# An encoder layer's second feed-forward projection: token-major Strassen products from streamed operands, with some operands stored as two planes

## The chip, the core and the metric

The kernel runs on one core of a Trainium2 chip. The metric is device time in microseconds (us) of one execution, input and output in the chip's memory (HBM). Engines: TensorE (PE) does matmuls into PSUM, VectorE (DVE), ScalarE (ACT) and GpSimd (POOL) do elementwise work, SyncE (SP) issues nearly all DMAs. Each engine works through its own instructions in a fixed order; an instruction waits on semaphores for what it needs, and everything behind it on that engine waits with it.

## What is computed

One layer of an encoder, float32, 2048 tokens of 1024 features, 16 query heads and 4 key heads, window of 128, hidden size 2816:

```python
h = rmsnorm(x, mix_norm_pre) * (1 + sc1) + sh1
y = windowed_gqa_sink(h, w_qkv, w_o, sink, rel_bias)
x = x + g1 * rmsnorm(y, mix_norm_post)
h = rmsnorm(x, ffn_norm_pre) * (1 + sc2) + sh2
a, b = split(h @ w_in, 2);  y = (silu(a) * b) @ w_out
x = x + g2 * rmsnorm(y, ffn_norm_post)          # rmsnorm: y * rsqrt(mean(y*y, -1) + eps) * gain
```

The change is about the last two lines: the product with `w_out` (2816 x 1024) and the norm, gain and residual behind it. `x` on the right of the last line is the result of the attention part, kept in HBM as `x1_d`.

## The kernel before

Matmuls take operands in a rounded 32-bit form (`fp32r`). For full precision each operand is split: `split` lets ScalarE copy it to the rounded high part and VectorE subtract that from the original to get the low part (lines 149 and 150). A product is then three matmuls, high x high, high x low, low x high (`three`, lines 144 to 146). A matmul has a stationary operand of 128x128 and a moving one of up to 128x512, and fills a PSUM buffer of 128x512.

The feed-forward part works by Strassen's scheme with seven products for 2x2 blocks. The two halves of 1024 tokens (`hf` 0 and 1) are two chunks of 512 tokens each (`CPH` = 2), and these are the two columns of the blocks.

*First projection (hidden phase).* For every half and 22 blocks of `w_in` (`Hidden`, names ending `_i0_t`, `_i1_t`) seven products of 12 matmuls go to PSUM tiles `pc0` to `pc6` of the pool `psC`, which has six buffers. ScalarE copies product 0 to `p1`; VectorE adds the others into `u2`, `p1`, `u3`, `b1` (lines 803 to 822). Then SiLU (line 828) and a product on GpSimd (line 832) give the hidden activations. Two neighbouring blocks are a pair (11 a half); `give_pair` forms the seven right-hand Strassen operands of the pair (`b11`, `b21`, `b22` as they are, `t1` to `t4` by two subtractions on GpSimd and two on VectorE) and stores each as 128x512 floats in `g_d`. The temporaries come from a pool of ten buffers, `tmp`. In half 0 the last two blocks are done product by product in turn (`interleaved`), while the operands of half 1 (`hb..`, `ht..`) are loaded and split as those of half 0 come free. The raw `w_in` tiles, their four sums on GpSimd (`s1` to `s4`) and the splits (`wa..`, `ws..`) are made a block or two ahead.

*Second projection.* It is cut along the hidden dimension into parts, `PARTS`: of each half four parts with 2, 3, 3, 3 and 3, 3, 3, 2 pairs, written (hf, part). The class `Outs` does all parts but the last: `w_out` is the stationary operand and the activations move, so the output has features on partitions. The part's activation operands are loaded from `g_d` and split (names like `hb21o0_1_0`), and for each of four pairs of feature blocks (`n2`) the rows `wiro` of `w_out` are loaded, their sums made and split. Product i goes to `pc{i}_o..` in `psC`; in a half's first part ScalarE copies it to a sum tile `z` (line 960), later VectorE adds it (line 963). In the half's last Strassen part the seven sums are combined (`COMBINE`, line 967). The last part, (1,3), is done without Strassen (`pl`, 96 matmuls with 512 columns and 192 with 256). The norm squares on ScalarE (line 993), adds squares on GpSimd or VectorE (line 994), sums over features by matmuls with ones, and multiplies (line 1010) and adds the residual (line 1011, `zx`).

The order on every engine is set when the kernel is built, by a scheduler that takes the program's order as its priority, with `tc.high_priority` moving pieces earlier. The last hidden block does its steps 0 to 4, then the first loads of the second projection are put in with high priority, then its steps 5 and 6.

## Time and profile before

| | us |
|---|---|
| runs | 2222.78, 2218.33, 2224.84 (median 2222.78) |
| profiled execution | 2223.03 |
| its span, first to last instruction | 2221.2 |
| VectorE, ScalarE, GpSimd busy | 1619.7, 1083.4, 1226.4 |
| mean granted TensorE clock | 0.967 of full speed |

All times below are from the profiled execution, counted from the span's start. In groups of instructions a line reads: line, engine, operation, tile written and tiles read, shapes, count, then total busy time and mean ns of one, then how long its engine was idle before it and what ended that. A row of a window gives its span, then the busy time of each engine with the number of instructions. The second projection runs from about 1724 to the end.

### The profile page before, as it was taken

The page shows a single profiled execution, that of the slowest core. Times are in us where ns is not written, and L with a number is a line of the kernel's source. Part 1 is how long each engine was busy: PE and PEld are TensorE (multiplying, and loading weights), DVE is VectorE, ACT ScalarE, POOL GpSimd, SP SyncE. Part 2 cuts the span into 40 slices and gives each one's busy share as a digit, 9 for nine tenths or more (in the row PEclk, how much of TensorE's full clock was granted, in tenths as well). Part 3 has the DMA queues.
Part 4 walks back from the last instruction along what each step waited for, and adds up shares of the span by engine and source line. Part 5 has one row for each costly group of instructions (what it writes and reads, how often), then busy time and mean ns, then how long its engine had stood idle before and what let it go on. Part 6 is the DMA issues. An engine that isn't in the chain of part 4 may idle for free.

```text
span 2221.2 us, 29169 instructions
## 1 busy us (share of the span) xinstructions
PE 2072.4 (93%) x9366; PEld 1672.9 (75%) x9366; DVE 1619.7 (73%) x2546; ACT 1083.4 (49%) x2153; POOL 1226.4 (55%) x1093
## 2 busy tenths in 40 slices
...
GB/s 260 236 263 302 259 172 220 147 209 167 182 207 157 181 216 99 174 143 152 158 184 172 241 189 114 103 106 105 89 101 79 206 157 151 119 105 256 161 128 100
DMA packets 263493, 375.97 MB, mean 169 GB/s; under 512 B 86011, under 2 KB 138796, under 8 KB 261292
## 3 DMA queue, kind: packets, MB, share of 16 engines
...
q10 hardware_dynamic: 576, 0.52, 0.1%
HBM read 263.37 MB, written 110.66 MB: 168 GB/s over the span
## 4 chain that ended last, share of the span: by engine, by line
PE 32%; DVE 8%; DMA 4%; issue 3%; POOL 3%; ACT 1%; SPq 0%; DVEq 0%; POOLq 0%; ACTq 0%
PE pc_i L145 6%; PE pc_i L144 6%; PE pc_i L146 6%; PE pc_o L145 4%; PE pc_o L144 4%; PE pc_o L146 4%; DMA wiri<-w_in 1%; DVE z L963 1%; DVE zx L1011 1%; DVE ws_o L150 1%; DMA ly<-y_d 1%; POOL z L967 1%; DMA lh<-x_d 1%; DVE ly L522 0%; DVE z L967 0%
## 5 line engine op out<-in xcount | busy, mean ns | idle before, releaser
L144 PE MATMUL pc_i<-ht,ws_i 128*128 128x512 f32 x528 | 208.6, 395 | 1.6 <-DVE u_i L806 0.9
L146 PE MATMUL pc_i<-ht,ws_i 128*128 128x512 f32 x528 | 207.2, 392 | 0.0
L145 PE MATMUL pc_i<-ht,ws_i 128*128 128x512 f32 x528 | 207.0, 392 | 0.0
L459 POOL TENSOR_SCALAR pr<-pr,rs 128x288 f32<-128x288 f32 (+3 forms) x256 | 138.5, 561 | 66.9 <-DVE rs L457 61.6
L453 DVE CUSTOM_DVE_ANT_0 pr<-s,bias,nsink 128x288 f32<-128x288 f32 (+3 forms) x256 | 123.8, 499 | 66.1 <-PE s L450 54.0
L455 ACT ACTIVATE pr<-pr,nm 128x289 f32<-128x289 f32 (+3 forms) x256 | 135.5, 532 | 73.6 <-DVE nm L453 63.7
L150 DVE TENSOR_TENSOR wa_i<-wiri,wa_i 128x512 fp32r<-128x512 f32 x132 | 135.1, 1024 | 38.9 <-ACT wa_i L149 33.3
L832 POOL TENSOR_TENSOR p_i<-p_i,u_i 128x512 f32<-128x512 f32 x44 | 69.9, 1589 | 168.3 <-DVE u_i L819 106.9
L150 DVE TENSOR_TENSOR ws_i<-s_i,ws_i 128x512 fp32r<-128x512 f32 x132 | 128.5, 973 | 27.4 <-ACT ws_i L149 25.7
L149 ACT CAST ws_i<-s_i 128x512 fp32r<-128x512 f32 x132 | 81.7, 621 | 134.2 <-PE pc_i L146 126.3
L145 PE MATMUL pc_i<-hb,wa_i 128*128 128x512 f32 x352 | 140.0, 398 | 2.6 <-DVE hb L150 2.6
L146 PE MATMUL pc_i<-hb,wa_i 128*128 128x512 f32 x352 | 140.2, 398 | 2.0 <-DVE wa_i L150 2.0
L144 PE MATMUL pc_i<-hb,wa_i 128*128 128x512 f32 x352 | 141.0, 400 | 0.4 <-DVE b_i L816 0.4
L149 ACT CAST wa_i<-wiri 128x512 fp32r<-128x512 f32 x132 | 81.9, 621 | 118.3 <-PE pc_i L146 115.8
L450 PE MATMUL s<-k,q 128*128 128x288 f32 (+4 forms) x512 | 116.4, 327 | 19.8 <-DVE nm L453 19.5
L472 PE MATMUL t<-ident,pr 128*128 128x128 f32 x736 | 119.0, 285 | 14.4 <-DVE plo L150 6.0
L150 DVE TENSOR_TENSOR plo<-t,phi 128x512 fp32r<-128x512 f32 x184 | 122.1, 683 | 14.1 <-ACT phi L149 12.9
L144 PEld LDWEIGHTS pc_i<-ht,ws_i 128*128 128x128 f32 x528 | 99.8, 189 | 24.5 <-DVE u_i L806 1.4
L450 PEld LDWEIGHTS s<-k,q 128*128 128x128 f32 x512 | 88.0, 201 | 39.3 <-DVE nm L453 28.8
L146 PEld LDWEIGHTS pc_i<-ht,ws_i 128*128 128x128 f32 x528 | 99.4, 188 | 23.2
L472 PEld LDWEIGHTS t<-ident,pr 128*128 128x128 f32 x736 | 92.7, 146 | 32.0 <-POOL pr L462 7.7
L145 PEld LDWEIGHTS pc_i<-ht,ws_i 128*128 128x128 f32 x528 | 99.4, 188 | 22.6 <-DVE ht L150 0.4
...
## 6 DMA issues: line engine op xcount, KB each, us to landing
...
q_d<-eq SPq DMA_DIRECT2D x64, 256.0 KB, 4.9
q<-q_d SPq DMA_DIRECT2D x16, 1024.0 KB, 6.1
...
g_d_b<-p_i SPq DMA_DIRECT2D x44, 256.0 KB, 4.9
```

What stands on the lines that cost most here:

```text
L144: pe.matmul(ps, w[0], h[0], start=first, stop=False)
L145: pe.matmul(ps, w[0], h[1], start=False, stop=False)
L146: pe.matmul(ps, w[1], h[0], start=False, stop=last)
L149: act.copy(hi, src)
L150: return eng.tensor_tensor(lo, src, f(hi), ALU.subtract).ins
L450: m = pe.matmul(ps[:, :n], qs, kk[:, e, jb * P + lo:jb * P + hi], start=e == 0, stop=e == 1)
L453: dve.tensor_tensor_reduce(pr[:, i, lo:hi], ps[:, :n], bias[g][:, lo - starts[i]:hi - starts[i]], -1.0, nsink[:, g:g + 1], ALU.add, ALU.mi ...
L455: act.activation(pr[:, i, lo:hi + 1], pr[:, i, lo:hi + 1], AF.Exp, bias=nm[:, i:i + 1], scale=-1.0, accum_out=rs[:, i:i + 1])
L459: pool.tensor_scalar(pr[:, i, lo:hi], pr[:, i, lo:hi], rs[:, i:i + 1], 1.0, ALU.mult, ALU.mult)
L472: pe.transpose(pt[:, i * P:(i + 1) * P], pr[:, i, jj * P:(jj + 1) * P], ident)
L832: pool.tensor_tensor(sa, sa, b, ALU.mult)
L963: dve.tensor_tensor(q, ps, q, ALU.add)
```

## The change

What it does:

- `give_pair` stores 14 of the 22 pairs (parts (0,3) and all of half 1, `SPLIT`) as two planes, high and low. For each of a pair's seven operands ScalarE now makes the high part (`gh..`) and VectorE the low part (`gl..`, or in place), in the hidden phase, and two DMAs store them; the tiles come from the same ten buffers. The second projection then loads both planes in one DMA and does not split them. The other eight pairs are stored and split as before.
- All eight parts go by Strassen, and the last pair of blocks is interleaved in both halves. The steps 5 and 6 of the last hidden block no longer lie between the loads.
- The activations are the stationary operand (128 tokens) and the `w_out` blocks move (512 features), so a PSUM tile `po` holds tokens on partitions. `Weights.put` loads a pair's rows of `w_out` as one tile of 1 MB (`wr`), makes the sums on GpSimd and splits them; the raw tile has one buffer for each of the three pairs. `Grams.load` streams the activations into 15 buffers, product by product. Order: part, product, token block b; in the last part token block, then product.
- Norm: ScalarE squares with an accumulated sum along the row (`ss`), a few short operations on 128x2 numbers give the factor `r`, and one VectorE operation multiplies with `r` and the gain row `grow`. The residual `x1` is loaded as it is and turned by 16 TensorE transposes for a token block (`px`); a VectorE addition ends it. `out` is written token-major.

The diff, cut to its core (the removed class `Outs`, the removed last part and the old norm are left out):

```diff
+SPLIT = ((0, 3), (1, 0), (1, 1), (1, 2), (1, 3))
...
-    g_d = [[{n: dram.tile([P, CH], F32, name=f"g_d{i}_{j}_{n}") for n in OPERANDS + ("b12",)}
+    part_of = [[(p, k) for p, m in enumerate(PARTS[i]) for k in range(m)] for i in range(S // HALF)]
+    g_d = [[{n: dram.tile([P, 2 if (i, part_of[i][j][0]) in SPLIT else 1, CH], F32, name=f"g_d{i}_{j}_{n}") for n in OPERANDS}
...
     def give_pair(hf, j):
         b = {f"b{e + 1}{i + 1}": hidden.pop((2 * j + e, i)) for e in range(2) for i in range(CPH)}
-        def give(n, t):
-            sp.dma_start(g_d[hf][j][n], t)
-        if hf == S // HALF - 1 and j >= HT // 2 - PARTS[-1][-1]:
-            for n in b:
-                give(n, b[n])
-        else:
-            differences(b["b11"], b["b12"], b["b21"], b["b22"], give)
+        parted = (hf, part_of[hf][j][0]) in SPLIT
+        def give(n, t, keep):
+            d = g_d[hf][j][n]
+            if not parted:
+                sp.dma_start(d[:, 0], t)
+                return
+            hi = temp(f"gh{hf}_{j}_{n}").bitcast(F32R)
+            lo = (temp(f"gl{hf}_{j}_{n}") if keep else t).bitcast(F32R)
+            split(hi, lo, t, dve)
+            sp.dma_start(d[:, 0], f(hi))
+            sp.dma_start(d[:, 1], f(lo))
+        b11, b12, b21, b22 = (b[n] for n in ("b11", "b12", "b21", "b22"))
+        give("b11", b11, True)
+        pool.tensor_tensor(b11, b12, b11, ALU.subtract)
+        dve.tensor_tensor(b12, b22, b12, ALU.subtract)
+        give("t3", b12, False)
+        give("b22", b22, True)
+        pool.tensor_tensor(b22, b22, b11, ALU.subtract)
+        give("t1", b11, False)
+        give("b21", b21, True)
+        dve.tensor_tensor(b21, b21, b22, ALU.subtract)
+        give("t2", b22, False)
+        give("t4", b21, False)
...
-        for t in range(HT - 2 if hf + 1 < S // HALF else HT - 1):
+        for t in range(HT - 2):
...
+        pair = [Hidden(half, t, hf) for t in range(HT - 2, HT)]
+        half = None
         if hf + 1 < S // HALF:
-            pair = [Hidden(half, t, hf) for t in range(HT - 2, HT)]
...
-            interleaved(pair, half)
-    hid = Hidden(half, HT - 1, hf)
-    for i in range(5):
-        hid.step(i)
+        interleaved(pair, half)
     early.close()
...
+    ffn.close()
+    psc.close()
...
+    PRODUCTS = (("s1", "t1", "5"), ("a12", "b21", "2"), ("a11", "b11", "1"), ("s2", "t2", "6"),
+                ("a22", "t4", "4"), ("s3", "t3", "7"), ("s4", "b22", "3"))
+    SUMS = {"1": (("2", "1", pool),), "6": (("6", "1", dve), ("1", "6", "5", pool)),
+            "7": (("7", "6", dve), ("4", "7", pool), ("5", "7", dve)), "3": (("3", "1", dve),)}
...
+    WB, GB, G0 = 14, 15, 5
...
+    psO = open_pool(ctx, "psO", 6, space=PSUM)
+    parts = [(hf, p) for hf in range(S // HALF) for p in range(len(PARTS[hf]))]
+    stages = [(part, i) for part in parts for i in range(len(PRODUCTS))]
+    class Weights:
+        def __init__(self):
+            self.at, self.n, self.src, self.w = 0, 0, [], {}
+        def load(self, hf, p):
+            self.src = []
+            for k in range(PARTS[hf][p]):
+                u = f"{hf}_{p}_{k}"
+                j = sum(PARTS[hf][:p]) + k
+                raw = rp.tile([P, 2, 2, CH], F32, tag=f"raw{k}", name=f"wr{u}")
+                sp.dma_start(raw, a["w_out"][2 * j:2 * j + 2].rearrange("e p (i c) -> p e i c", i=2))
+                a11, a12, a21, a22 = [raw[:, e, i] for i in range(2) for e in range(2)]
+                s1 = rp.tile([P, CH], F32, tag=f"s{k}", name=f"ws{u}")
+                pool.tensor_tensor(s1, a21, a22, ALU.add)
+                pool.tensor_tensor(a21, a11, a21, ALU.subtract)
+                self.src.append(dict(a11=a11, a12=a12, a22=a22, s1=s1, s2=s1, s3=a21, s4=a12))
+        def put(self, n=1):
...
+                (hf, p), i = stages[self.at]
+                self.at += 1
+                if i == 0:
+                    self.load(hf, p)
+                name = PRODUCTS[i][0]
+                for k, src in enumerate(self.src):
+                    t = wo.tile([P, 2, CH], F32R, tag=f"w{self.n % WB}", name=f"wo{hf}_{p}_{name}_{k}")
+                    self.n += 1
+                    split(t[:, 0], t[:, 1], src[name], dve)
+                    self.w[hf, p, i, k] = t
+                    if name == "s1":
+                        pool.tensor_tensor(src["s2"], src["s1"], src["a11"], ALU.subtract)
+                    elif name == "a12":
+                        pool.tensor_tensor(src["s4"], src["a12"], src["s2"], ALU.subtract)
+    class Grams:
+        def __init__(self):
+            self.at, self.n, self.g = 0, G0, {}
+        def load(self, n=1):
...
+                (hf, p), i = stages[self.at]
+                self.at += 1
+                for k in range(PARTS[hf][p]):
+                    d = g_d[hf][sum(PARTS[hf][:p]) + k][PRODUCTS[i][1]]
+                    t = gp.tile([P, 2, CH], F32R, tag=f"g{self.n % GB}", name=f"g{hf}_{p}_{i}_{k}")
+                    self.n += 1
+                    if (hf, p) in SPLIT:
+                        sp.dma_start(f(t), d)
+                    else:
+                        sp.dma_start(f(t[:, 1]), d[:, 0])
+                        split(t[:, 0], t[:, 1], f(t[:, 1]), dve)
+                    self.g[hf, p, i, k] = t
...
+    def product(hf, p, i, b):
+        m, name = PARTS[hf][p], PRODUCTS[i][2]
+        ps = psO.tile([P, CH], F32, tag="p", name=f"po{hf}_{p}_{i}_{b}")
+        for k in range(m):
+            g, w = grams.g[hf, p, i, k][:, :, b * P:(b + 1) * P], wts.w[hf, p, i, k]
+            pe.matmul(ps, g[:, 0], w[:, 0], start=k == 0, stop=False)
+            pe.matmul(ps, g[:, 0], w[:, 1], start=False, stop=False)
+            pe.matmul(ps, g[:, 1], w[:, 0], start=False, stop=k == m - 1)
+        if p == 0:
+            z[hf, b, name] = yp.tile([P, CH], F32, tag="z", name=f"z{hf}_{b}_{name}", bufs=28)
+            act.copy(z[hf, b, name], ps)
+        else:
+            dve.tensor_tensor(z[hf, b, name], ps, z[hf, b, name], ALU.add)
+        if p == len(PARTS[hf]) - 1:
+            for x, *y, eng in SUMS.get(name, ()):
+                y = [x] + y if len(y) == 1 else y
+                eng.tensor_tensor(z[hf, b, x], z[hf, b, y[0]], z[hf, b, y[1]], ALU.add)
...
+    def finish(hf, b):
+        x1, ss = {}, yp.tile([P, 4], F32, tag="ss", name=f"ss{hf}_{b}", bufs=2)
+        for j in range(CPH):
+            x1[j] = yp.tile([P, KT, P], F32, tag="x1", name=f"x1_{hf}_{j}_{b}", bufs=2)
+            sp.dma_start(x1[j], x1_d[hf * CPH + j][:, :, b * P:(b + 1) * P])
+            for i in range(2):
+                sq = yp.tile([P, CH], F32, tag="sq", name=f"sq{hf}_{j}_{b}_{i}", bufs=1)
+                act.activation(sq, z[hf, b, PLACE[i, j]], AF.Square, accum_out=ss[:, i * 2 + j:i * 2 + j + 1])
+        yield
...
+        yield
+        for j in range(CPH):
+            for i in range(2):
+                y = z[hf, b, PLACE[i, j]]
+                px = psF.tile([P, CH], F32, tag="mm", name=f"px{hf}_{j}_{b}_{i}")
+                for k in range(JB):
+                    pe.transpose(px[:, k * P:(k + 1) * P], x1[j][:, i * JB + k, :], ident)
+                dve.scalar_tensor_tensor(y, y, r[:, j:j + 1], grow[:, i * CH:(i + 1) * CH], ALU.mult, ALU.mult)
+                dve.tensor_tensor(y, px, y, ALU.add)
+                sp.dma_start(out[hf * CPH + j, b, :, i * CH:(i + 1) * CH], y)
...
+    wts, grams = Weights(), Grams()
...
+        grams.load(4)
+        wts.put(4)
...
+    for hf, p in parts[:-1]:
+        for i in range(len(PRODUCTS)):
+            for b in range(JB):
+                product(hf, p, i, b)
+                next(end, None)
+            wts.put()
+            grams.load()
+        if p == len(PARTS[hf]) - 1:
+            end = chain(*(finish(hf, b) for b in range(JB)))
+    for b in range(JB):
+        for i in range(len(PRODUCTS)):
+            product(*parts[-1], i, b)
+            if b == 0:
+                wts.put()
+                grams.load()
+            next(end, None)
+        end = chain(end, finish(parts[-1][0], b))
+    for _ in end:
+        pass
```

What the scheduler makes of it. First, ScalarE at the seam between the halves: `p1_i0_20` is the copy of product 0 of half 0's block 20, `gh0_9_..` are high parts of pair 9 (blocks 18 and 19), `hb111_..` operands of half 1. Before:

```order
L828 ACTIVATE u2_i0_19_11993<-u2_i0_19_11993 128x512
L803 COPY p1_i0_20_12180<-pc0_i0_20_12167 128x512
L149 CAST wa11_i1_0_12514<-wiri1_0_12504 128x512
L803 COPY p1_i0_21_12195<-pc0_i0_21_12182 128x512
L149 CAST wa11_i1_1_12652<-wiri1_1_12642 128x512
L149 CAST ws2_i1_0_12517<-s2_i1_0_12508 128x512
L149 CAST hb111_0_12197<-hb111_0_12197 128x512
L149 CAST hb111_1_12201<-hb111_1_12201 128x512
```

and now:

```order
L152 CAST gh0_9_t1_12102<-p1_i0_18_11828 128x512
L152 CAST gh0_9_b21_12107<-p1_i0_19_11988 128x512
L152 CAST hb111_0_12238<-hb111_0_12238 128x512
L152 CAST wa11_i1_1_12724<-wiri1_1_12714 128x512
L152 CAST hb111_1_12242<-hb111_1_12242 128x512
L152 CAST ws2_i1_0_12589<-s2_i1_0_12580 128x512
L152 CAST gh0_9_t2_12114<-u2_i0_19_12003 128x512
L152 CAST gh0_9_t4_12119<-p1_i0_19_11988 128x512
L152 CAST ws2_i1_1_12727<-s2_i1_1_12718 128x512
L152 CAST hb111_2_12246<-hb111_2_12246 128x512
L152 CAST hb111_3_12250<-hb111_3_12250 128x512
L823 COPY p1_i0_20_12221<-pc0_i0_20_12208 128x512
```

The copy now stands behind the last of pair 9's high parts and four operands of half 1; before, it stood ahead of these operands.

Second, ScalarE at the start of the second projection, around its first copies out of PSUM (`z`). Before, with `wa..`, `ws..` parts of the third group of rows `wiro0_0_2`:

```order
L149 CAST wa11_o0_0_2_15924<-wiro0_0_2_15914 128x256
L149 CAST hb22o0_0_0_15749<-hb22o0_0_0_15749 128x512
L149 CAST hb22o0_0_1_15753<-hb22o0_0_1_15753 128x512
L149 CAST ws2_o0_0_2_15927<-s2_o0_0_2_15918 128x256
L960 COPY z0_0_0_15764<-pc0_o0_0_0_15757 128x512
L960 COPY z0_0_1_15773<-pc1_o0_0_0_15766 128x512
L960 COPY z0_0_2_15782<-pc2_o0_0_0_15775 128x512
L960 COPY z0_0_3_15791<-pc3_o0_0_0_15784 128x512
```

and now, with `gh1_10_..` high parts of the very last pair, `g0_1_..` operands of part (0,1), and `wo0_1_s1_..` that part's first sums of `w_out`:

```order
L152 CAST gh1_10_t4_16069<-p1_i1_21_15846 128x512
L1085 ACT_TABLE_LOAD
L152 CAST g0_1_0_1_16392<-g0_1_0_1_16392 128x512
L152 CAST wo0_1_s1_0_16376<-ws0_1_0_16363 128x512
L152 CAST g0_1_0_2_16396<-g0_1_0_2_16396 128x512
L152 CAST wo0_1_s1_1_16380<-ws0_1_1_16368 128x512
L1050 COPY growt_16171<-pgrow_16169 8x128
L1036 COPY z0_0_5_16182<-po0_0_0_0_16175 128x512
L1036 COPY z0_1_5_16191<-po0_0_0_1_16184 128x512
L1036 COPY z0_2_5_16200<-po0_0_0_2_16193 128x512
```

The copies now stand behind pieces that belong to the next part. The raw tiles that `wo0_1_s1_0` and `wo0_1_s1_1` come from are loaded into the buffers of part (0,0), `wr0_0_0` and `wr0_0_1`, after VectorE has split the last sum made there, and the load of `wr0_0_0` itself waits for the last matmul of the hidden phase, whose operands lay in that room. On SyncE the loads of `wr0_1_0` and `wr0_1_1` stand behind the stores of pair 10's planes.

Third, VectorE at the end of the program. Before:

```order
L136 TENSOR_TENSOR nrz3_256_19994<-nrz3_256_19994,ntz3_256_20004 128x256
L1010 TENSOR_TENSOR z1_0_6_17941<-z1_0_6_17941,nrz3_256_19994 128x256
L1010 TENSOR_TENSOR z1_1_6_18126<-z1_1_6_18126,nrz3_256_19994 128x256
L1010 TENSOR_TENSOR z1_2_6_18426<-z1_2_6_18426,nrz3_256_19994 128x256
L1010 TENSOR_TENSOR z1_3_6_18438<-z1_3_6_18438,nrz3_256_19994 128x256
L1011 SCALAR_TENSOR_TENSOR zx3_0_19651<-z1_0_6_17941,coef_336,zx3_0_19651 128x256
L1011 SCALAR_TENSOR_TENSOR zx3_1_19669<-z1_0_4_17897,coef_336,zx3_1_19669 128x256
L1011 SCALAR_TENSOR_TENSOR zx3_2_19688<-z1_1_6_18126,coef_336,zx3_2_19688 128x256
L1011 SCALAR_TENSOR_TENSOR zx3_4_19742<-z1_2_6_18426,coef_336,zx3_4_19742 128x256
L1011 SCALAR_TENSOR_TENSOR zx3_3_19717<-z1_1_4_18082,coef_336,zx3_3_19717 128x256
```

and now:

```order
L1072 TENSOR_TENSOR r1_3_19955<-r1_3_19955,t1_3_19956 128x2
L1080 SCALAR_TENSOR_TENSOR z1_3_2_18169<-z1_3_2_18169,r1_3_19955,grow_16097 128x512
L1080 SCALAR_TENSOR_TENSOR z1_3_4_18504<-z1_3_4_18504,r1_3_19955,grow_16097 128x512
L1080 SCALAR_TENSOR_TENSOR z1_3_3_18633<-z1_3_3_18633,r1_3_19955,grow_16097 128x512
L1080 SCALAR_TENSOR_TENSOR z1_3_5_18050<-z1_3_5_18050,r1_3_19955,grow_16097 128x512
L1081 TENSOR_TENSOR z1_3_2_18169<-px1_0_3_0_19965,z1_3_2_18169 128x512
L1081 TENSOR_TENSOR z1_3_4_18504<-px1_0_3_1_19973,z1_3_4_18504 128x512
L1081 TENSOR_TENSOR z1_3_3_18633<-px1_1_3_0_19981,z1_3_3_18633 128x512
L1081 TENSOR_TENSOR z1_3_5_18050<-px1_1_3_1_19989,z1_3_5_18050 128x512
```

The last token block's four scaled tiles and four residual additions from PSUM now end the program, where there were pieces of 256 columns scaled and added.

189 lines of the change are left out of this document (38 added, 151 removed).

## The prediction

> **What bounds the kernel now.** I read the page first, then windows by stage, then the groups and the chain of waits at the places that the change touches.
>
> ```profile
> span 2221.2 us, 29169 instructions
> PE 2072.4 (93%) x9366; PEld 1672.9 (75%) x9366; DVE 1619.7 (73%) x2546; ACT 1083.4 (49%) x2153; POOL 1226.4 (55%) x1093
> PE 32%; DVE 8%; DMA 4%; issue 3%; POOL 3%; ACT 1%; SPq 0%; DVEq 0%; POOLq 0%; ACTq 0%
> ```
>
> TensorE is busy 93% of the span and has the largest share of the chain that ended last, so what can change is the 149 us in which it is not busy, and the number of matmuls. By window the columns are: us, TensorE busy (matmuls), weight loads, VectorE, ScalarE, GpSimd, granted clock, DMA share, GB/s.
>
> ```profile
> 1250.00:1270.00 20.00, 20.00 (x88) 16.20 (x87) 13.62 (x15) 7.86 (x14) 16.31 (x13) 1.00 0.83 271
> 1270.00:1320.00 50.00, 44.42 (x178) 34.12 (x177) 49.09 (x64) 28.02 (x52) 24.50 (x16) 0.93 0.63 223
> 1400.00:1460.00 60.00, 60.00 (x262) 48.91 (x261) 37.02 (x47) 18.99 (x31) 32.33 (x23) 1.00 0.30 101
> 1730.00:1780.00 50.00, 48.56 (x201) 38.71 (x202) 40.07 (x60) 40.49 (x86) 17.96 (x17) 0.97 0.60 201
> 1780.00:1930.00 150.00, 150.00 (x648) 121.55 (x648) 131.15 (x194) 63.98 (x123) 66.22 (x52) 1.00 0.42 134
> 1930.00:2080.00 150.00, 128.61 (x513) 96.87 (x512) 143.43 (x171) 74.57 (x148) 89.23 (x63) 0.97 0.55 186
> 2080.00:2130.00 50.00, 50.00 (x217) 40.52 (x216) 49.54 (x71) 20.07 (x40) 27.65 (x20) 1.00 0.35 111
> 2180.00:2222.00 42.00, 24.53 (x172) 23.03 (x170) 35.76 (x60) 9.86 (x23) 18.15 (x16) 0.81 0.39 132
> ```
>
> The hidden phase (1400 to 1460) is full on TensorE with VectorE at 62%. Two places lose: the seam between the halves (1270 to 1320: VectorE 49 of 50 us, TensorE 5.6 us idle), and the second projection, where VectorE is full from 1930 to 2080 and TensorE idles 21.4 us, plus 17.5 us in the tail. The hidden matmuls, pc_i, end at 1724.3:
>
> ```profile
> 1700.00:1724.00 24.00, 24.00 (x105) 19.35 (x103) 5.74 (x9) 0.58 (x1) 1.00 0.45 153
> 1724.00:1726.00 2.00, 0.31 (x2) 0.00 (x0) 0.88 (x2) 0.00 (x0) 1.00 0.00 0
> ```
>
> So the second projection lasts 2221.2 - 1724.3 = 497 us.
>
> **1. The seam between the halves: +15 us (6 to 22).** Each pair with two planes costs 7 casts, 7 subtractions and 7 more DMAs. Their nearest rows, from the second half's hidden blocks on (DMA row: whole run):
>
> ```profile
> L150 DVE TENSOR_TENSOR ws_i<-s_i,ws_i 128x512 fp32r<-128x512 f32 x64 | 57.1, 892 | 1.8 <-ACT ws_i L149 0.3
> L149 ACT CAST ws_i<-s_i 128x512 fp32r<-128x512 f32 x62 | 38.6, 624 | 111.1 <-PE pc_i L146 103.7 <-POOL s_i L761 3.7 <-POOL wiri L763 2.2
> L719 POOL TENSOR_TENSOR u_i<-u_i,p_i 128x512 f32<-128x512 f32 x10 | 13.8, 1383 | 0.0
> g_d_b<-p_i SPq DMA_DIRECT2D x44, 256.0 KB, 4.9
> ```
>
> Pair 8 of half 0 falls where VectorE has room. Pairs 9 and 10 put 14 subtractions x 0.892 = 12.5 us into the stretch where VectorE has 0.9 us free in 50. In the changed order the ScalarE copy of the first product of block 20, which frees a PSUM buffer, and VectorE's addition of the second stand behind pair 9's splits, and the buffers of the planes come back only when their DMA has landed, 4.9 us. The queued DMAs of pair 9 also go out ahead of the late residual's loads, so the last operands of half 1 come late. I take 12.5 + about half such a landing, 15. Lower end: pair 9 fits the 6.4 us that VectorE has free from 1250 to 1270, 12.5 - 6.4 = 6. Upper end: both in line with a whole landing and one more GpSimd subtraction at 1.4 for each pair, 12.5 + 4.9 + 2.8 = 20, and 2 for the clock, 0.93 there: 22. In half 1 the same work is 7 x 0.892 = 6.2 us for a pair, whose 168 matmuls last 60 / 262 x 168 = 38.5 us: VectorE goes from 62% to 78%. I cost that at nothing; the cover is the six PSUM buffers.
>
> **2. Matmuls of the second projection: 425.8 us.** 1848 of 128x512 (11 pairs x 7 x 3 x 4 blocks x 2 halves), at 50 / 217 = 0.2304 from the window 2080 to 2130. Before it was 1680 and the 96 plus 192 half-wide of the classical part. There are now no ones-matmuls for the norm.
>
> **3. Its start: +29 us lost (14 to 36).** Rows: the load nearest in size, the load on the chain, GpSimd and ScalarE after it, the split's second half, the PSUM copy, the first matmul.
>
> ```profile
> q<-q_d SPq DMA_DIRECT2D x16, 1024.0 KB, 6.1
> 1708.58 5.84 DMA wiro<-w_out
> 1714.55 0.76 POOL s_o L761
> 1732.40 0.79 PE pc_o L144
> L761 POOL TENSOR_TENSOR s_o<-wiro 128x384 f32<-128x384 f32 x24 | 29.7, 1238 | 130.1 <-DVE ws_o L150 119.6 <-DMA hb22o<-g_d_b 7.3 <-DMA wiro<-w_out 3.2
> L150 DVE TENSOR_TENSOR wa_o<-wiro,wa_o 128x384 fp32r<-128x384 f32 x72 | 65.1, 904 | 0.2 <-ACT wa_o L149 0.2
> L960 ACT COPY z<-pc_o 128x512 f32<-128x512 f32 x56 | 32.5, 595 | 16.7 <-DVE zx L1011 11.4 <-PE pc_o L146 5.2
> ```
>
> Before, the first w_out load was issued at 1708.6, under hidden matmuls. Now the first 1 MB load takes room that the last hidden product still reads, so it starts at t0, the end of the hidden phase: landed at t0 + 6.5. From there VectorE has 23 splits and small jobs in line until the fourth sum of both tiles is split, 23 x 0.904 = 20.8, t0 + 27.3. Only then is the raw tile free for the second part's rows: +6.1, then GpSimd's sum, 1.2, and the cast, 0.6: t0 + 35.3. ScalarE has that cast ahead of its first PSUM copy, 0.6, so the six PSUM buffers come free from t0 + 36. Before that TensorE can do 36 matmuls, 8.3 us: 27.7 lost. The window 1730 to 1780 granted 0.97 of the clock after its wait, 1.5 us in 50: 29. The lower end, 14, has the copies unhindered: 6.5 landed, 1.2 + 0.6 + 0.9 to the first operands, 4 until the second tile is split. The upper, 36, prices the 23 splits at 1.2 (as GpSimd's row). The pages speak of that clock: the Trainium skill's "TensorE: Matmul & The Clock Gate" (What's actually happening) has an idle window of some 3.4 us halve the clock and as long a busy one restore it; with two waits here that is 3.4 us instead of 1.5, and the sum would be 1.9 us later.
>
> **4. The middle: +9.6 and +4 (2 to 8).** The token-major x1 goes through 64 transposes inside the second half. The nearest row is four of them in 0.60 us; 64 x 0.15 = 9.6, all on TensorE.
>
> ```profile
> 605.07 0.60 PE L472 MATMUL t<-ident,pr 128*128 128x128 f32 x4
> L963 DVE TENSOR_TENSOR z<-pc_o,z 128x512 f32<-128x512 f32 x140 | 95.5, 682 | 18.4 <-PE pc_o L146 18.4
> L967 DVE TENSOR_TENSOR z<-z,z 128x512 f32<-128x512 f32 x24 | 22.8, 950 | 0.1
> 2196.90 0.66 DVE zx L1011
> L967 POOL TENSOR_TENSOR z<-z,z 128x512 f32<-128x512 f32 x32 | 48.7, 1540 | 36.3 <-DVE z L963 18.7 <-DVE z L967 17.6
> out<-zx SPq DMA_DIRECT2D x24, 256.0 KB, 2.9
> ```
>
> A part of three pairs lasts 252 x 0.2304 = 58 us. In the first half's second part VectorE has 28 additions x 0.682 and 42 splits x 0.904, 57 of 58: as full as 1780 to 1930, which lost nothing. From (0,3) on there is nothing left to split of g: (0,3) has 19.1 + 21 x 0.904 + 16 sums x 0.95 = 53. So the 21.4 us lost from 1930 to 2080 go. The 32 squares with their sums go on ScalarE, 64 of 150 us busy there, and the 98 products' second planes add 98 x 256 KB to loads whose DMA share is 0.35 to 0.55: nothing for both, VectorE being fuller. What stays is the finish of half 0 in (1,0), 16 x 0.66 + 16 x 0.682 = 21.5 more on VectorE, 59.6 of 58, and GpSimd beside it: 4.
>
> **5. The tail: +27 us (21 to 33).** The last part, (1,3), goes block by block, and VectorE has 28 x 0.682 + 16 x 0.95 + 16 x 0.66 + 16 x 0.682 + 24 short ones at some 0.15 = 59 us of work there against 168 x 0.2304 = 38.7 on TensorE. With 1.4 until the first product, 2 for the square's way through ScalarE in the last block and 2.9 for the last store, the end is 66 after the part's start: +27. Before, GpSimd and the pieces of 256 were waited for in its place. The lower end takes the sums at 0.68 and two us of waits fewer; the upper the sums at 1.2.
>
> GpSimd has 12 sums in that part. The Trainium skill's "SBUF — State Buffer" (Who interferes with whom) says that a VectorE operation with two SBUF inputs and a GpSimd one that reads SBUF lock each other out for a whole instruction; the two L967 rows, 950 and 1540, show both drawn out. Were VectorE shut out of the sums for all of it, 12 x 0.76 = 9 us would come on top: that is the fourth rival.
>
> **The sum.** 1724.3 + 15 + 425.8 + 29 + 9.6 + 4 + 27 = 2234.7. The profiled execution took 2223.03 at a span of 2221.2, so 1.8 on top: 2236.5, call it 2237; the median of the runs, 2222.78, is the profiled execution's within 0.3.
>
> **Rivals.**
> - Faster, 2205 to 2215: the two queue orders cost little, because ScalarE and VectorE run ahead of what the rows allow, and the relief of the full stretch decides: 1724.3 + 6 + 425.8 + 14 + 9.6 + 4 + 25 + 1.8 = 2210.5. For it speaks that the changed matmul work is no larger and 21 us of VectorE waits go. Against it: the first raw load cannot start before the hidden phase ends. It decides when seam and start together stay under 23 us.
> - No change, about 2222: seam 8, start 22, rest as forecast.
> - The hidden phase starves: if the planes' buffers come back late in half 1, each of its 11 pairs loses 1 to 2 us: 2250 to 2260. Speaks for it: ten buffers now also wait 4.9 us for DMAs; against: 22% of VectorE stays free.
> - The tail with VectorE and GpSimd taking turns: 2246.
>
> **How the numbers follow.** 0.3% of 2222.8 is 6.7 us, about what a measurement here can tell from no change. Forecast case 0.34, starving 0.08, taking turns 0.10: slower 0.52. No change 0.22. Faster 0.26. The range from all lower ends (1724.3 + 6 + 425.8 + 14 + 9.6 + 2 + 21 + 1.8 = 2204.5) to all upper ends (22, 36, 8, 33: 2260.5) is cut at the far end by a little: 2205 to 2258. Within the forecast case alone it is 2230 to 2246.
>
> **What would show it.** Right: TensorE with 10 us or more idle from 1260 to 1330; after the last hidden matmul two gaps, the second ended by a ScalarE copy of a z tile, with some 36 matmuls between them; no VectorE-full window in the second half's middle parts; a last part of about 66 us with VectorE at 90%. Wrong: PSUM copies of the first product within 20 us of the hidden end; hidden windows of half 1 under 58 of 60; or a last part under 55 us.

## The result, and the profile after

| | before | after |
|---|---|---|
| median of the runs on the same chip (4 each) | 2222.61 | 2249.66 |
| profiled execution, its span | 2223.03, 2221.2 | 2245.18, 2243.4 |
| mean granted TensorE clock | 0.967 | 0.959 |

The ratio is 1.0122, 95% interval 1.0100 to 1.0143: slower by 27 us. The forecast said slower, 2237, range 2205 to 2258; it was 12.7 us too low. From the page after, the span and the engines:

```profile
span 2243.4 us, 28903 instructions
...
PE 2062.5 (92%) x9351; PEld 1674.8 (75%) x9351; DVE 1645.6 (73%) x2554; ACT 1077.6 (48%) x2135; POOL 1154.7 (51%) x1018
```

TensorE has 10 us less work and the span is 22 us longer, so some 32 us of idle time came in. By window, columns as before:

```profile
1167.60:1251.00 83.40, 80.22 (x341) 64.60 (x340) 65.90 (x76) 35.58 (x58) 56.93 (x39) 0.98 0.58 199
1250.00:1270.00 20.00, 17.83 (x77) 14.08 (x76) 17.23 (x19) 7.77 (x14) 16.07 (x11) 1.00 0.75 269
1270.00:1320.00 50.00, 41.26 (x168) 32.91 (x168) 49.42 (x64) 29.16 (x53) 23.32 (x15) 0.93 0.74 258
1320.00:1340.00 20.00, 11.31 (x39) 9.03 (x40) 16.32 (x20) 7.38 (x14) 12.47 (x8) 0.66 0.56 203
1400.00:1460.00 60.00, 60.00 (x261) 48.80 (x260) 49.51 (x60) 24.34 (x42) 32.38 (x22) 1.00 0.42 152
1740.00:1790.00 50.00, 15.62 (x45) 10.46 (x44) 40.55 (x42) 26.10 (x48) 29.91 (x20) 0.67 0.75 271
1934.00:1991.00 57.00, 57.00 (x253) 47.21 (x252) 43.50 (x51) 13.02 (x24) 33.78 (x22) 1.00 0.69 249
1991.00:2062.00 71.00, 66.78 (x315) 54.67 (x314) 52.12 (x94) 35.91 (x85) 19.82 (x14) 0.98 0.84 304
2176.50:2217.20 40.70, 40.70 (x192) 33.64 (x190) 37.78 (x64) 10.13 (x29) 11.62 (x9) 1.00 0.27 90
2217.20:2243.40 26.20, 8.74 (x41) 6.65 (x40) 21.24 (x40) 3.48 (x12) 4.25 (x3) 0.64 0.54 180
```

Three places lose: the end of half 0 with the four blocks ahead of it (the first four rows), the start of the second projection (1740 to 1790: TensorE 15.6 of 50), and the end. The middle is as wanted: in part (0,3), 1934 to 1991, TensorE is full and VectorE is not. TensorE's waits (who waited, on whom, us in total, times, longest) at the last four blocks of half 0 that come singly, at its end, at the start and in the last part:

```profile
PE pc_i L147 <- ACT p_i L823: 3.0, 1, 3.0
```

```profile
PE pc_i L147 <- ACT p_i L823: 17.1, 2, 10.4
PE pc_i L148 <- DVE ht L153: 2.5, 1, 2.5
```

```profile
PE po L1031 <- ACT z L1036: 17.9, 1, 17.9
PE po L1031 <- ACT wo_s L152: 11.0, 1, 11.0
```

```profile
PE px L1079 <- DVE z L1081: 9.7, 3, 5.2
PE px L1079 <- DMA x<-x_d: 3.3, 1, 3.3
```

The waits of 17.1 and 17.9 are for ScalarE copies that empty a PSUM buffer; the 17.1 are one of 6.7 and one of 10.4. Was ScalarE busy? The timeline ahead of the second one's end, ScalarE with two subtractions on VectorE (start, us, what; in brackets the idle time before and what ended it):

```profile
1317.39 0.68 DVE L804 TENSOR_TENSOR u_i<-u_i,u_i 128x512 f32<-128x512 f32 x1
...
1318.11 0.62 ACT L152 CAST gh_t<-u_i 128x512 fp32r<-128x512 f32 x1 [6.20 <-DVE u_i L804]
...
1324.04 0.62 ACT L152 CAST gh_t<-u_i 128x512 fp32r<-128x512 f32 x1 [2.20 <-POOL u_i L807]
...
1325.71 1.74 DVE L810 TENSOR_TENSOR p_i<-p_i,u_i 128x512 f32<-128x512 f32 x1
...
1327.53 0.62 ACT L152 CAST gh_t<-p_i 128x512 fp32r<-128x512 f32 x1 [2.35 <-issue]
1328.06 0.58 ACT L823 COPY p_i<-pc_i 128x512 f32<-128x512 f32 x1
```

It was not: it stood idle 6.2, 2.2 and 2.4 us in front of casts of pair 10's high parts, whose inputs VectorE and GpSimd had not yet made, and the copy that TensorE needs stood behind them. (The first wait, 6.7, ends the same way behind pair 9's, with ScalarE idle 3.9 and 2.2.) VectorE, however, was full: in the whole stage, 1251 to 1334, it was busy 78.0 of 83.0 us, in the kernel before 59.3 of 66.6. It came to the subtraction at 1317.39 only 7.8 us after GpSimd had made the last input (1309.56), with splits of half 1's operands and weights in between.

### The profile page after: what moved, and what is told of

The parts are those of the page before. It is cut to its first block, busy times and chain, and to the rows that moved or that the text cites. A ratio compares the mean times of both kernels' runs of the same rounds, so it can differ in the third digit from the quotient of the medians.

```text
span 2243.4 us, 28903 instructions
## 1 busy us (share of the span) xinstructions
PE 2062.5 (92%) x9351; PEld 1674.8 (75%) x9351; DVE 1645.6 (73%) x2554; ACT 1077.6 (48%) x2135; POOL 1154.7 (51%) x1018
## 4 chain that ended last, share of the span: by engine, by line
PE 32%; DVE 8%; POOL 4%; issue 4%; DMA 3%; ACT 2%; SPq 0%; POOLq 0%; DVEq 0%; ACTq 0%
PE pc_i L147 6%; PE pc_i L148 6%; PE pc_i L149 6%; PE po L1031 4%; PE po L1033 4%; PE po L1032 4%; DVE z L1042 1%; DMA wr<-w_out 1%; DVE z L1038 1%; DVE z L1080 1%; DVE wo_s L153 1%; DVE wo_a L153 1%; DMA ly<-y_d 1%; DVE wa_i L153 1%; POOL ws L979 0%
## 5 line engine op out<-in xcount | busy, mean ns | idle before, releaser
L456 DVE CUSTOM_DVE_ANT_0 pr<-s,bias,nsink 128x288 f32<-128x288 f32 (+3 forms) x256 | 123.5, 497 | 66.8 <-PE s L453 55.4
L458 ACT ACTIVATE pr<-pr,nm 128x289 f32<-128x289 f32 (+3 forms) x256 | 135.2, 530 | 74.0 <-DVE nm L456 65.2
L153 DVE TENSOR_TENSOR wa_i<-wiri,wa_i 128x512 fp32r<-128x512 f32 x132 | 148.9, 1128 | 21.4 <-ACT wa_i L152 21.4
L1038 DVE TENSOR_TENSOR z<-po,z 128x512 f32<-128x512 f32 x168 | 113.5, 684 | 51.6 <-PE po L1033 50.1
L153 DVE TENSOR_TENSOR ws_i<-s_i,ws_i 128x512 fp32r<-128x512 f32 x132 | 136.6, 1035 | 19.4 <-ACT ws_i L152 19.2
L1031 PE MATMUL po<-wo_s,g 128*128 128x512 f32 x352 | 137.5, 394 | 11.6 <-ACT wo_s L152 11.0
L1032 PE MATMUL po<-wo_s,g 128*128 128x512 f32 x352 | 138.2, 393 | 4.0 <-DVE wo_s L153 4.0
L1033 PE MATMUL po<-wo_s,g 128*128 128x512 f32 x352 | 138.0, 392 | 0.0
L979 POOL TENSOR_TENSOR ws<-wr 128x512 f32<-128x512 f32 x22 | 32.2, 1464 | 195.4 <-DMA wr<-w_out 195.4
L153 DVE TENSOR_TENSOR plo<-t,phi 128x512 fp32r<-128x512 f32 x184 | 121.9, 681 | 14.7 <-ACT phi L152 13.6
```

What stands on the lines that cost most here:

```text
L153: return eng.tensor_tensor(lo, src, f(hi), ALU.subtract).ins
L456: dve.tensor_tensor_reduce(pr[:, i, lo:hi], ps[:, :n], bias[g][:, lo - starts[i]:hi - starts[i]], -1.0, nsink[:, g:g + 1], ALU.add, ALU.mi ...
L458: act.activation(pr[:, i, lo:hi + 1], pr[:, i, lo:hi + 1], AF.Exp, bias=nm[:, i:i + 1], scale=-1.0, accum_out=rs[:, i:i + 1])
L1031: pe.matmul(ps, g[:, 0], w[:, 0], start=k == 0, stop=False)
L1032: pe.matmul(ps, g[:, 0], w[:, 1], start=False, stop=False)
L1033: pe.matmul(ps, g[:, 1], w[:, 0], start=False, stop=k == m - 1)
```

## The experiments

No experiment leaves out any work. Line numbers move by up to six from kernel to kernel. Stage lengths in us, each from its first and last matmul in the trace: "16 to 20" runs from block 16's first matmul to block 20's in half 0; "end of half 0" from there to the end of half 1's block 0; "half 1" from there to the last hidden matmul; "start" from there to the end of part (0,0), whose 168 matmuls take 38.1 undisturbed; "last part" from the end of (1,2) to the span's end. Parts not listed took 57.1 everywhere. Each ratio is to the kernel before as timed on the same chip (medians 2222.61 to 2225.26). The stages come from one profile each; where kernels do the same in a stage they still differ, by up to 4 us in "16 to 20" (80.5 to 84.9 with pair 8 as two planes) and 3.5 in "end of half 0" (82.6 to 86.1).

| kernel | median | ratio to before, 95% | 16 to 20 | end of half 0 | half 1 | start | (0,3) | (1,0) | last part |
|---|---|---|---|---|---|---|---|---|---|
| before | 2222.61 | | 78.0 | 66.6 | 408.0 | | | | |
| after | 2249.66 | 1.0122 [1.0100, 1.0143] | 83.4 | 83.0 | 407.0 | 79.1 | 57.1 | 70.8 | 66.9 |
| e1 | 2248.64 | 1.0112 [1.0099, 1.0125] | 84.9 | 82.6 | 407.0 | 78.0 | 57.1 | 69.8 | 67.5 |
| e2 | 2243.39 | 1.0087 [1.0074, 1.0100] | 81.1 | 86.1 | 407.0 | 70.9 | 57.1 | 69.2 | 67.2 |
| e3 | 2234.11 | 1.0045 [1.0033, 1.0057] | 81.3 | 68.0 | 413.3 | 73.1 | 57.1 | 71.5 | 66.8 |
| e4 | 2259.82 | 1.0162 [1.0149, 1.0175] | 83.9 | 83.2 | 407.0 | 78.3 | 57.1 | 80.5 | 65.8 |
| e5 | 2226.55 | 1.0016 [1.0005, 1.0026] | 79.5 | 66.5 | 408.8 | 63.5 | 62.6 | 77.9 | 67.0 |
| e6 | 2225.29 | 1.0010 [0.9999, 1.0021] | 83.6 | 66.7 | 413.4 | 65.2 | 57.1 | 71.2 | 67.1 |
| e7 | 2222.97 | 0.9997 [0.9987, 1.0006] | 83.2 | 64.8 | 415.0 | 63.0 | 57.1 | 72.5 | 67.4 |
| e8 | 2251.41 | 1.0124 [1.0106, 1.0143] | 81.6 | 85.4 | 407.1 | 78.8 | 57.1 | 70.5 | 67.7 |
| e9 | 2235.62 | 1.0048 [1.0034, 1.0062] | 80.5 | 84.4 | 407.0 | 62.9 | 57.1 | 69.0 | 66.7 |
| e10 | 2219.80 | 0.9989 [0.9978, 1.0000] | 82.1 | 64.0 | 413.9 | 61.0 | 57.1 | 71.2 | 66.2 |
| e11 | 2216.37 | 0.9962 [0.9947, 0.9976] | 84.2 | 63.5 | 408.3 | 62.1 | 57.1 | 71.0 | 66.3 |
| e12 | 2210.92 | 0.9937 [0.9922, 0.9952] | 78.0 | 66.8 | 408.3 | 60.6 | 57.1 | 70.6 | 66.0 |

**e1: the order on ScalarE at the start.**

```diff
+            if (hf, p, i) == (0, 0, 1):
+                behind = last[0].ins
-            wts.put()
-            grams.load()
+            with tc.issue_after(behind) if (hf, p) == (0, 0) and i >= 3 else ExitStack():
+                wts.put()
+                grams.load()
```

> The changed kernel, but ScalarE's pieces of part (0,1) are queued behind the copies of products 0 and 1 of part (0,0). Theory A (the copies only stand behind these pieces in ScalarE's queue): TensorE's second wait at the start, 17.9 us, ends when ScalarE has done the last pair's splits and the table load, at about 1773 instead of 1788: 14 us faster than the changed kernel, about 2235. Theory B (the z tiles and the gain row also lie where the last pair's temporaries lay, whose stores are issued until 1778): the copies wait until about 1782, so 5 to 6 us faster, about 2244. Rival C: VectorE, full in part (0,1), takes the gain back later: no change.

The start was 78.0 and the wait hardly moved:

```profile
PE po L1031 <- ACT z L1036: 16.3, 1, 16.3
```

```profile
1791.19 3.04 ACT L1036 COPY z<-po 128x512 f32<-128x512 f32 x6 [8.20 <-DMA g_d_t<-u_i]
```

The copies no longer stood behind part (0,1)'s casts, but now they waited for room, 8.2 us for a store of the last pair's planes: the first `z` tile and the tile of the gain row lie over `tmp`, until those planes have been stored. So theory B named the wait, but not its length: the copies came at 1791, not 1782. The order was not the bottleneck by itself.

**e2: the order and the room.** As e1, with the gain row made after part (0,0) and its tile put ahead of the `z` tiles, so that the first `z` tile lies elsewhere.

```diff
+    rowt = yp.tile([P, CH], F32, tag="z", name="growt", bufs=29)[:KT, :P]
...
+        if (hf, p) == (0, 0):
+            make_row()
```

> As e1_order, and the first z tile and the gain row moved off the last pair's temporaries (one more z buffer, the row made after part (0,0)). Theories A and B together: the copies start at about 1773, 14 us faster than the changed kernel, about 2235. Rival C (VectorE takes it back): 2245 or more.

```profile
PE po L1031 <- ACT z L1036: 7.3, 2, 4.4
```

The start fell to 70.9. The copies came 31.3 us after the last hidden matmul instead of 46.6; of these 15 us, 8 reached the end of the stage. The wait for the first copies is the 4.4; the copies of product 2 now met part (0,1)'s casts (a second wait, 2.9, with matmuls at half their pace behind it). The time, 2243, lies between the two that were expected. The room without the order was not run.

**e3: pairs 9 and 10 of half 0 stored whole.** A list `WHOLE` exempts pairs from the two planes; they are split after loading, as the other eight are.

```diff
+WHOLE = ((0, 9), (0, 10))
...
+    def split_pair(i, j):
+        return (i, part_of[i][j][0]) in SPLIT and (i, j) not in WHOLE
...
-        parted = (hf, part_of[hf][j][0]) in SPLIT
+        parted = split_pair(hf, j)
...
-                    if (hf, p) in SPLIT:
+                    if split_pair(hf, sum(PARTS[hf][:p]) + k):
```

> The changed kernel, with pairs 9 and 10 of half 0 stored whole again, so that 12 of 22 pairs are stored as two planes. Theory (the 14 splits of these pairs cost the seam): TensorE's idle time from 1250 to 1340 falls from about 29 to about 6 us and the hidden phase ends near 1726 instead of 1741; part (0,3) gets 14 splits back on VectorE, 53 + 12.6 = 66 us of work for 58, so 8 us of it are lost again: about 2242, 7 faster than the changed kernel. Rival (the late residual's loads and the changed order at the seam cost it, not the splits): the seam keeps 10 us or more and the time is 2249 or above.

The end of half 0 fell from 83.0 to 68.0. Its waits, then those of the start:

```profile
PE pc_i L151 <- DVE u_i L830: 4.3, 1, 4.3
...
```

```profile
PE po L1035 <- ACT wo_s L156: 13.1, 1, 13.1
PE po L1035 <- ACT z L1040: 12.3, 1, 12.3
```

The copy of product 0 no longer appears. The edit takes pair 9's and 10's casts off ScalarE and their subtractions off VectorE (busy 59.2 of 68.0 us there now), so it does not show which of the two was enough to cause the loss. The operands of two of part (0,3)'s three pairs are now split in the second projection, and the part lost nothing, where 8 us were expected. Half 1 became 6 us longer, which e11 takes up.

**e4: the gain on GpSimd in the finish.** GpSimd multiplies by the gain row, and one VectorE operation scales and adds the residual from PSUM.

```diff
+                pool.tensor_tensor(y, y, grow[:, i * CH:(i + 1) * CH], ALU.mult)
...
-                dve.scalar_tensor_tensor(y, y, r[:, j:j + 1], grow[:, i * CH:(i + 1) * CH], ALU.mult, ALU.mult)
-                dve.tensor_tensor(y, px, y, ALU.add)
+                dve.scalar_tensor_tensor(y, y, r[:, j:j + 1], px, ALU.mult, ALU.add)
```

> The changed kernel, with the gain multiplied in on GpSimd ahead of the factor, and one VectorE operation (y times factor plus the residual from PSUM) instead of two. Theory (VectorE's 59 us of work bound the last part): 16 x 0.68 = 11 us less of it, the last part 8 us shorter, and 2 us in (1,0): about 2240. Rival (GpSimd and VectorE lock each other out, so the 32 more GpSimd operations stretch VectorE's sums and GpSimd becomes late): the last part keeps its 67 us or grows, 2249 or above.

In the last part (groups of instructions):

```profile
L1064 POOL TENSOR_TENSOR z<-z,grow 128x512 f32<-128x512 f32 x16 | 20.8, 1319 | 6.4 <-ACT sq L1063 6.4
L1082 DVE SCALAR_TENSOR_TENSOR z<-z,r,px 128x512 f32<-128x512 f32 x16 | 11.4, 740 | 1.0 <-PE px L1081 0.6
```

VectorE lost its second operation, GpSimd's 1.3 us took its place: the last part gained 1.1, and part (1,0) lost 9.7. Slower in all.

**e5: every pair stored whole.**

```diff
-SPLIT = ((0, 3), (1, 0), (1, 1), (1, 2), (1, 3))
+SPLIT = ()
```

> The changed kernel with all 22 pairs stored whole, so every activation operand is split in the second projection. Theory (after e3_seam: VectorE has room in the middle parts, a split costs it 0.6 to 0.8 us there): the seam falls back by 15 us, parts (0,3) to (1,2) keep their 57 and 71 us, and only the last part, which VectorE bounds, grows by its 14 splits, about 8 us: about 2243. Rival (the prediction's arithmetic, 0.904 us for a split on a VectorE that is full): (0,3) and (1,0) grow by 14 and 21 us, the last part by 13: about 2280.

It is 23 us faster than the changed kernel. Both expectations were missed; neither had named the start. The four blocks, the end of half 0 and the start come out 3.9, 16.5 and 15.6 shorter. Parts (0,3) and (1,0) give back 5.5 and 7.1, by their windows:

```profile
1902.00:1964.50 62.50, 59.17 (x254) 47.98 (x253) 56.57 (x68) 23.80 (x42) 34.89 (x22) 0.97 0.42 140
1964.50:2042.40 77.90, 69.48 (x318) 55.60 (x317) 71.76 (x118) 46.82 (x107) 21.75 (x14) 0.96 0.61 205
```

VectorE is over 90% busy there. From the last hidden matmul to the span's end it takes 499.4 us (2223.3 - 1723.9), where the old projection took 496.9: the token-major Strassen part without planes costs 2.5 us, and the rest of the slowdown is that of the two planes.

**e6: e3 with the start rearranged.** `WHOLE` as in e3, room as in e2, part (0,1)'s casts behind the copies of product 3 instead of product 1 (the line against e2's).

```diff
-            if (hf, p, i) == (0, 0, 1):
+            if (hf, p, i) == (0, 0, 3):
```

> e3_seam's storing, the room of e2_order_room, and ScalarE's pieces of part (0,1) queued behind the copies of products 0 to 3, not 0 and 1. Theory (in e2_order_room the wait moved to product 2's copies, which still stood behind part (0,1)): from the last hidden matmul to the end of part (0,0) 64 us instead of 71 to 73, one wait less: about 2225, 9 faster than e3_seam. Rival (part (0,1)'s operands now come too late, or VectorE's splits bound the start anyway): the stage keeps 70 us or part (0,1) grows over 58: 2232 or more.

The start went from 73.1 to 65.2, and the time to the 2225 that was expected; the wait for `z` fell to 3.2, and the first wait, 13.0, stayed.

**e7: the weights earlier.** As e6, with the first raw weight tiles over memory that is free earlier, and their loads asked for ahead of the operands'.

```diff
+            self.pre = {k: (rp.tile([P, 2, 2, CH], F32, tag=f"raw{k}", name=f"wr0_{int(k == 2)}_{k}"),
+                            rp.tile([P, CH], F32, tag=f"s{k}", name=f"ws0_{int(k == 2)}_{k}")) for k in (2, 1, 0)}
...
-        grams.load(4)
         wts.put(4)
-        make_row()
+        grams.load(4)
```

> e6_start, and the raw w_out tiles placed so that the first two lie where early-used weights of the last hidden block lay, their loads put ahead of the activation loads. Theory (the first wait, 10 to 13 us, is the 1 MB load that could not start before the last hidden matmul): it shrinks by 5 to 6 us, about 2220. Rival (VectorE, busy without a pause for 35 us at the start, is what both waits hang on): no change against e6_start.

Start 63.0, first wait 10.1. By the medians this is 2.3 us less than e6, but the two intervals overlap, so a gain is not shown. From its chain of waits, where the first two loads were held:

```profile
1731.73 0.32 SPq L804
...
1735.50 8.87 DMA wr<-w_out
```

On SP's queue the loads still stood behind a store of a low part of half 1's last pair (L804), which waits for the last blocks' results, and six operand loads; they went out 1.0 and 0.4 us before the last hidden matmul ended (1735.9). More room does not help a load that stands in line behind a late store.

**e8: sums to GpSimd in the last part.**

```diff
+                if (hf, p) == parts[-1] and b < JB - 1:
+                    eng = pool
                 eng.tensor_tensor(z[hf, b, x], z[hf, b, y[0]], z[hf, b, y[1]], ALU.add)
```

> The changed kernel with all seven sums of the last part's token blocks 0 to 2 on GpSimd. Theory (VectorE's work bounds the last part, and it does not slow on additions from PSUM while GpSimd works): 12 x 0.95 = 11 us less on VectorE, the last part 6 to 9 us shorter than its 67: about 2242. Rival (as in e4_tail, GpSimd becomes late, 21 + 3 sums at 1.5 us and more): 67 us or more, 2249 or above.

```profile
L1044 POOL TENSOR_TENSOR z<-z,z 128x512 f32<-128x512 f32 x24 | 31.4, 1325 | 36.1 <-DVE z L1038 33.1 <-DVE r L1074 1.0 <-DVE v L1068 0.8
L1082 DVE SCALAR_TENSOR_TENSOR z<-z,r,grow 128x512 f32<-128x512 f32 x16 | 14.1, 941 | 0.2
```

The scaling on VectorE, 0.75 us apiece in the changed kernel, rose to 0.94 beside the busier GpSimd, and the last part took 67.7 instead of 66.9. Relieving VectorE by way of GpSimd does not shorten the end.

**e9: only the last two pairs of half 1 whole**, nothing else changed.

```diff
+WHOLE = ((1, 9), (1, 10))
```

> The changed kernel with only the last two operand pairs of half 1 (numbers 9 and 10) stored whole; the pairs of half 0 and the other pairs of half 1 stay high and low parts, and no queue is reordered. Theory (what delays the PSUM copies at the start of the projection is above all VectorE's and the DMA queues' work for the parts of the last pairs): the stage from the last hidden matmul to the end of part (0,0) falls from 79 to 62-66 us, the end of half 0 stays at 83 us, the last part at 67 us; in all 2231-2238 us, ratio 1.003-1.006. Rival (the start is set by the 1 MB loads and by the order of ScalarE's casts, whatever the pairs are stored as): the stage stays at 75-79 us and the time at 2245-2250 us. Should both parts of the loss at half 0 and at the start hang together (a shorter start only where half 0 is shorter as well), the stage would stay above 70 us.

```profile
PE po L1035 <- ACT wo_s L156: 11.0, 1, 11.0
PE po L1035 <- ACT z L1040: 4.5, 1, 4.5
```

```profile
1772.96 2.96 ACT L1040 COPY z<-po 128x512 f32<-128x512 f32 x6
...
1781.29 1.14 ACT L156 CAST wo_s<-ws 128x512 fp32r<-128x512 f32 x2
```

The start fell from 79.1 to 62.9, the end of half 0 stayed. The wait for the `z` copy fell from 17.9 to 4.5. So 16 us of the start hang on how the last two pairs are stored. But ScalarE's order did not stay: no line of the kernel reorders it, yet the scheduler now put the first `z` copies ahead of the casts of part (0,1)'s sums (1781.29), which stood ahead of them in the changed kernel. (In e3 the start came out 6 us shorter as well, with nothing edited there.) Up to the copies VectorE has 11.5 us less to do (28.0 us instead of 39.5). How much is due to the parts' work, to the room that their stores hold, and to this order is not separated; e1 and e2 show that the order alone is worth 1 us and order and room together 8.

**e10: both, with the early weights and a third x1 buffer.** Four pairs whole, e7's start (the gain row's tile now beside the `z` tiles and not one of them), and in the finish:

```diff
-            x1[j] = yp.tile([P, KT, P], F32, tag="x1", name=f"x1_{hf}_{j}_{b}", bufs=2)
+            x1[j] = yp.tile([P, KT, P], F32, tag="x1", name=f"x1_{hf}_{j}_{b}", bufs=3)
```

> The changed kernel with the last two pairs of both halves stored whole (four pairs), the first weight tiles of the projection put over earlier freed memory and asked for ahead of the first operand tiles, ScalarE's casts for part (0,1) behind the copies of product 3, the gain row made after part (0,0) and its tile ahead of the first z tiles, and three x1 buffers instead of two in the last part. Theory (the parts' work ahead of the start and the late weight load add up, and the last x1 load waits for a buffer): end of half 0 66-69 us, start 50-58 us, part (0,3) 57-58 us, part (1,0) 71-73 us, last part 62-64 us; in all 2206-2214 us, ratio 0.992-0.996, which beats both kernels. Rival 1 (the weight load stands behind the last stores of half 1 in SP's queue, and these are no earlier when stored whole): start 61-64 us, in all 2214-2220 us. Rival 2 (the last part is bound by VectorE, not by the x1 load): last part 66-67 us, 3-5 us more than the theory gives.

Both rivals held: the start came to 61.0, the last part to 66.2. In the last part the wait for the x1 load is gone and VectorE's has grown in its place; the other fence is a wait in half 1's block 2:

```profile
PE px L1085 <- DVE z L1087: 12.2, 4, 5.2
```

```profile
PE pc_i L151 <- ACT p_i L827: 4.2, 1, 4.2
```

**e11: half 1's first pair whole too.**

```diff
-WHOLE = ((0, 9), (0, 10), (1, 9), (1, 10))
+WHOLE = ((0, 9), (0, 10), (1, 0), (1, 9), (1, 10))
```

> The kernel of the run before (first pairs 9 and 10 of both halves whole, early weights, reordered casts, three x1 buffers) with pair 0 of half 1 stored whole as well. In that kernel half 1's hidden blocks 1 and 2 take 45 us from the first matmul of block 1 to that of block 3, where the changed kernel and the kernel before take 39, and the stage from the end of block 0 to the last hidden matmul 414 us instead of 407. Theory (the parts of half 1's first pair stand ahead of a PSUM copy on ScalarE and VectorE, which the shorter end of half 0 has moved onto TensorE's path): 407-409 us for that stage, the end of half 0 still 64-68; the pair's operands are then split in part (1,0), at 71-74 us; in all 2212-2217 us, ratio 0.995-0.998. Rival (the 6 us come from operands of half 1 that arrive late, not from the parts): 412-415 us for the stage, in all 2219-2223 us.

Half 1 took 408.3 instead of 413.9: the theory held. In e10, seven GpSimd operations in a row (1337 to 1349, chain of waits) come ahead of this pair's casts, ScalarE stands idle 3.1 and 5.3 us in front of two of them, and product 0's copy, for which TensorE waits 4.2, stands behind; now these casts are gone.

**e12: pair 8 of half 0 whole too.** `WHOLE` gets (0, 8), so only pairs 1 to 8 of half 1 are two planes.

> As e11, with pair 8 of half 0 stored whole too, so that only pairs 1 to 8 of half 1 are high and low parts. The time from block 16 to block 20 of half 0 is 78.0 us in the kernel before, 79.5 with all pairs whole, and 81 to 85 in the kernels in which pair 8 is split there. Theory 1 (pair 8 costs 3 us where it is given, and VectorE has room for its splits in part (0,3)): 78-80 us for the four blocks, part (0,3) 57-58, in all 1-4 us less than e11. Theory 2 (with pair 8's splits back, part (0,3) is full on VectorE, as with all pairs whole, where it took 62.6 us): four blocks 78-80, part (0,3) 61-63, in all e11 plus 1 to 4 us.

The four blocks took 78.0, as before the change. Part (0,3) with its three pairs split there:

```profile
1903.00:1960.00 57.00, 56.95 (x251) 46.58 (x249) 55.13 (x66) 19.44 (x35) 36.63 (x23) 1.00 0.55 190
```

VectorE is at 97% and TensorE still full, so theory 1 held by stage (the medians fell by 5.4, more than its 1 to 4). In e5, with about as much on VectorE in this part (56.6 us in 68 operations, against 55.1 in 66), TensorE waited once, 3.2 us, for an addition that frees a PSUM buffer and stood behind four drawn-out VectorE operations (6.2 us); with the granted clock at 0.97 over the part this makes up most of the 5.5. Why such a row of operations held TensorE there and not here is open. This version beats both kernels: 2210.92, 0.6% under the kernel before.

## Why the prediction was right and where not

In the profiled executions, against the prediction's terms (matmuls at the 57.1 us that 252 took in the changed kernel; every loss is what a stage took beyond its matmuls):

| term | forecast | measured |
|---|---|---|
| ahead of block 16 | 0 | -4.1 |
| blocks 16 to 20 (pair 8) | 0 | +5.4 |
| 1, end of half 0 | +15 | +16.4 |
| half 1 | 0 | -1.0 |
| 2, 1848 matmuls | 425.8 | 418.7 |
| 3, start | 29 | 41.0 |
| 4, part (1,0) | 13.6 | 13.7 |
| 5, last part | 27 | 28.8 |
| span | 2234.7 | 2243.4 (the terms give 2243.2) |

The direction and the three places were right. That the sum was only 8.7 us low is in part luck: 7.1 too many in step 2 and 4.1 by chance ahead of block 16 hide much of what the start and pair 8 cost more. The median, 2249.66, lies above the 2230 to 2246 of the forecast case alone.

- *Step 3, the start, is the one that was mis-sized*: it lost 41 where the term had 29 and 36 was its upper end. The links of the walk were there, as the chain of waits shows at its end:

```profile
1775.25 5.34 DMA wr<-w_out
1780.72 1.27 POOL ws L979
1782.01 0.63 ACT wo_s L152
...
1783.95 1.64 POOL ws L998
1785.60 1.23 POOL ws L979
...
1787.37 0.25 ACT growt L1050
1787.62 0.49 ACT z L1036
1788.15 0.79 PE po L1031
```

The copies began 46.6 us after the last hidden matmul (1741.0), where the walk had 35.3. The first load landed after 7.3 instead of 6.5, and ScalarE came to its first cast at 8.8, behind four high parts of the last pair. VectorE took 25.4 from there to the fourth sums instead of 20.8, with low parts of the last pair in its line. The 0.904 was the mean for pieces of 384 columns in the kernel before; of the 39 subtractions of 512 columns from 1741 to 1790, 25 took 0.68 and 12 took 1.6 to 1.8:

```profile
1766.02 0.68 DVE L153 TENSOR_TENSOR wo_s<-ws,wo_s 128x512 fp32r<-128x512 f32 x1
...
1768.90 1.76 DVE L153 TENSOR_TENSOR wo_s<-ws,wo_s 128x512 fp32r<-128x512 f32 x1
```

The second load landed after 5.3 instead of 6.1. And after it GpSimd did two more sums ahead of the second cast (1.64 and 1.23), then the gain row's copy came: 7.0 us to the first copy where the walk had 1.8. What the walk did not name is the last two pairs: stored whole (e9) they shorten the start by 16 us. Of "the two queue orders" ScalarE's alone is not the lever: e1 changed it and gained 1 us.
- *Step 1* had the size, 16.4, and the copy behind pair 9's splits. Its sum was VectorE's work, 12.5, and half a landing; the trace shows 18.7 us more on VectorE (78.0 against 59.3), and copies that wait in line on an idle ScalarE behind casts that wait for that full VectorE and for GpSimd. Whether VectorE's work alone would have cost as much is not shown. The same happened one pair earlier, where the step said that pair 8 falls where VectorE has room: VectorE was 79% busy there (65.9 of 83.4), the room was there, and TensorE still waited 3.0 for a copy. Whole pairs brought both stretches back: e3 the end of half 0, e5 and e12 the four blocks (79.5 and 78.0, against 80.5 to 84.9 in the eleven kernels with pair 8 as two planes).
- *Half 1 at nothing* was right for the changed kernel (60.00 of 60 at VectorE 49.5), and not in general: in e3, e6, e7 and e10, with the shorter end of half 0, half 1 took 413 to 415, and taking its first pair out (e11) gave 5.6 of it back.
- *Step 2*: 7 us too many. The window it came from held matmuls of the same size, 128x512, that started 0.232 apart; in the changed kernel's parts they start 0.227 apart. Why is open.
- *Step 4* was right in sum, its 4 by luck: it counted 28 VectorE additions in (1,0), but that is a half's first part, whose tiles ScalarE copies. VectorE was busy 52.1 of 71.0 there, not full; TensorE waited 4.3, the longest time 3.3 for the addition that frees a transposes' buffer. For (0,3) the step counted VectorE nearly full, 53 of 58; it was busy 43.5 of 57. The price of a split was not too high (its 18 splits took 0.98 each), but some of this part's splits, additions and sums ran before or after it (18 of 21, 24 of 28 and 9 of 16 ran inside), which left room for two whole pairs (e3) and even three (e12).
- *Step 5* was right: 66.9, VectorE 37.8 + 21.2 = 59.0 as forecast, though not piece by piece: the sums cost less and the 24 short ones more, 7.8 instead of 3.6. The fourth rival, VectorE and GpSimd taking turns there, did not show: the last part's sums on VectorE took 0.85 us each and not the 1.2 of the upper end. The Trainium skill's "SBUF — State Buffer" (Who interferes with whom) has a lock between them: the 0.68 and 1.76 us above agree, and so does e8; at the end GpSimd simply had little to do, 15.9 us of 66.9.
- *The clock*, after the wait of 10.4 us at the end of half 0 (chain of waits):

```profile
1328.69 0.80 PE pc_i L147
...
1333.32 0.43 PE pc_i L148
1333.75 0.25 PE pc_i L149
1333.99 0.23 PE pc_i L147
```

Matmuls ran at 0.43 us for 5.1 us, then at 0.23; after the start's second wait for 2.9 us, some 1.6 us lost, and not the 3.4 that were counted for two waits, since the second wait ended with a ScalarE copy, whatever the pace of the 36 matmuls before it. The Trainium skill's "TensorE: Matmul & The Clock Gate" (What's actually happening) has half the clock until one window of some 3.4 us has been busy; both stretches fit that within 2 us.
- *The signs* came as forecast: TensorE idle 19.6 us from 1260 to 1330; two gaps in the start, 11.0 and 17.9, with 36 matmuls between them and a `z` copy at the end of the second; no middle part with VectorE full; a last part of 66.9 with VectorE at 88%.
- *The rivals*: "faster" needed start and end of half 0 under 23 together; they took 57. "Starving" did not come: half 1 kept its pace.
- The medians differ by 4.9 us more than the profiled executions (27.0 against 22.1): that of the changed kernel was its lowest run. Block 16 began at 1167.6 in it, at 1171.7 in the kernel before and at 1169 to 1175 in all the others; so the first row of the table is most likely chance.
